# Stores behind later loads, and side work re-spread, in a decoder layer on one core

## Chip, cores and metric

One core of a Trainium2 chip runs the whole layer in one launch. The time is device microseconds from start to end of that launch; lower is better. Three runs of the kernel before took 2120.0, 2126.58 and 2126.95 us.

## What is computed

One decoder layer over 2048 tokens of width 1024 in fp32, shortened from the reference:

```python
mod = silu(c) @ w_ada + b_ada                       # 6 x 1024
h = rms_norm(x, g_mix) * (1 + scale1) + shift1
z, q, k, v = split(h @ w_in)                        # 1024 | 512 | 128 | 128
u, v_a = split(gelu(z)); out_a = u * (tril(w_s) applied per 128-token chunk to v_a, + b_s)
out_b = attention(rope(q), rope(k), v)              # window 128, 8 heads, 2 kv heads, sinks
x = x + gate1 * (concat(out_a, out_b) @ w_out)
h2 = rms_norm(x, g_ffn) * (1 + scale2) + shift2
x = x + gate2 * (relu(h2 @ w_ff1) ** 2 @ w_ff2)     # 1024 -> 4096 -> 1024
y = rms_norm(x, g_final)
```

## The kernel before

**Tiles.** The tokens go in four slabs of 512, features on the partitions. Every fp32 operand of a large product is split into a rounded part and a remainder (hi, lo), and each product of 128 x 128 by 128 x 512 is three matmuls (mm3, L298 to L300): hi hi, hi lo, lo hi. Splitting is one ACT pass (hi) and one DVE pass (lo): halve (L69, L70) and w_split (L265, L266).

**Order of the program.** The slabs pass through the input projection (in_qkv for q, k, v; in_vu for the gated unit), attention, mix_build (reading both mixers' outputs back and splitting them), out_proj, and the MLP. The MLP takes slabs in pairs (0, 1) and (2, 3) and uses a seven-product scheme in place of eight blocks: h2_build makes seven forms of the normalised activations, ffn_c the first product (16 feature blocks j of 7 products), ffn_d the second (products 1, 6, 5, 3, 7, 4, 2, each over 8 contraction steps c, so 56 steps of 24 matmuls). w2_early and w2_late form sums of blocks of the second weight and keep them in DRAM (w2d). ada_rest computes a later part of the modulation vector in halves of 512 outputs: eight loaded slices, each scaled by ACT (L168) and added by POOL (L170), then four matmuls of one column.

**Weaving.** Each stage is a generator. weave(main, side, per) runs `per` steps of the side after each step of the main; ratio, chain, zipped and part combine side generators. What is written in this order, each engine's instructions then stand in an order that a scheduler sets; issue_after makes one instruction stand behind another. Before, the first pair's ffn_d runs three side steps per c step: slab 2's attention, all of slab 3 up to its out_proj, then h2_build of the second pair; w2_late takes one step per c step from the fifth on.

**Queue and buffers.** All large transfers are issued by SP, in program order; an issue waits for its data (a store) or for a free buffer (a load), and what stands behind it waits too. Stores are issued where the data is made: split weights (w_keep, L278), mixer outputs (L538, L654), residuals (L690), q, k, v of slabs 2 and 3 (L414), the weight sums (L770 to L786). Tiles come from rings: t2 (9 of 512 columns), xl (4), wk (12 of 1024), m2 (60). Statistics of a slab are a column sum by matmul (L201), a power on POOL (L206), and a broadcast by matmul (L221).

Of the kernel before, what the change touches and what calls it, by code (L numbers as in the profile page):

```python
# [49 lines left out]
def hybrid_block(ctx, tc, x_l, c_l, pos, wada0, wada, vec, win, wsT, bs, sinks, wout, w1, w2, rope_c, y_l):  # L50
# [54 lines left out]
    def x_tile(s, k, tag_x=False):  # L105
        t = m2("xr", F32) if tag_x else sb.tile([P, T], F32, name="xt", tag="xl", bufs=NXL)
        nc.sync.dma_start(out=t, in_=x_l[s, k])
        return t
# [51 lines left out]
    def ada_rest(ci):  # L160
        for half in range(2):
            acc = t2("acc")
            for k in range(KT):
                if k % 2 == 0:
                    two = wk("adar", F32, [P, 2, T])
                    nc.sync.dma_start(out=two, in_=wada[ci - 2, half, k:k + 2].rearrange("k p t -> p k t"))
                raw = two[:, k % 2]
# [87 lines left out]
    def w_split(key, big=False, eng=dve):  # L255
        raw = wk("raw", F32)
        nc.sync.dma_start(out=raw, in_=(win if key[0] == "i" else wout)[key[1]])
# [15 lines left out]
    def w_keep(key, w):  # L273
        n = D // len(w.hi)
        kept[key] = [dram.tile([P, D], F32, name=f"k{key[0]}{key[1]}{q}", tag=f"k{key[0]}{key[1]}{q}") for q in "hl"]
        for d, ts in zip(kept[key], (w.hi, w.lo)):
            for i, t in enumerate(ts):
                nc.sync.dma_start(out=d[:, i * n:(i + 1) * n], in_=t.bitcast(F32))  # L278

    def w_load(key):  # L280
# [3 lines left out]
        for t, d in zip((hi, lo), kept[key]):  # L284
            nc.sync.dma_start(out=t.bitcast(F32), in_=d)
# [40 lines left out]
    def setup_mixers():  # L326
        for i in range(2):
# [8 lines left out]
            for t in (wh, wl):  # L336
                wspd.append(dram.tile([P, T], F32, name=f"wsp{len(wspd)}", tag=f"wsp{len(wspd)}"))
                nc.sync.dma_start(out=wspd[-1], in_=t.bitcast(F32).rearrange("p g c -> p (g c)"))
# [73 lines left out]
    def away(s, name, t):  # L412
        d = dram.tile([P, T], F32, name=f"{name}d{s}", tag=f"{name}d{s}")
        nc.sync.dma_start(out=d, in_=t)  # L414
        qkvd[s, name] = d

    def back(s, name, t):
        nc.sync.dma_start(out=t, in_=qkvd[s, name])
# [67 lines left out]
    def in_vu(s, h, st, u0=None):  # L486
        vts, us = {}, {}
        sgu = list(wsp)
        if s > 0:
            ts = [m2("wsp", F32R, [P, 4, P]) for _ in range(4)]  # L490
            for t, d in zip(ts, wspd):
                nc.sync.dma_start(out=t.bitcast(F32).rearrange("p g c -> p (g c)"), in_=d)
# [27 lines left out]
        def gate(p):  # L520
# [17 lines left out]
            nc.sync.dma_start(out=mixd[s][p], in_=sv)  # L538
# [19 lines left out]
    def attention(s, st):  # L558
# [82 lines left out]
        def stage_o(n):  # L641
# [4 lines left out]
            for i, (kb, pt) in enumerate(pts):  # L646
                for hl in range(2):
# [6 lines left out]
            nc.sync.dma_start(out=mixbd[s][:, a:a + HD, b * P:(b + 1) * P].rearrange("j p c -> p j c"),  # L654
                              in_=os_[a:a + HD])
# [14 lines left out]
    def mix_build(s, mix):  # L670
        for k in range(KT):
            t = sb.tile([P, T], F32, name="xt", tag="xl", bufs=NXL)
            nc.sync.dma_start(out=t, in_=mixd[s][k] if k < 4 else mixbd[s][k - 4])
# [7 lines left out]
    def out_proj(s, mix):  # L681
        stat = Stat()
        for d in range(KT):
# [6 lines left out]
            nc.sync.dma_start(out=x2d[s][d], in_=x2)  # L690
# [21 lines left out]

    def h2_build(p, forms):
        for s in (2 * p, 2 * p + 1):
            rb2[s].diag()
        yield
        for s in (2 * p, 2 * p + 1):
            rb2[s] = rb2[s].cast()
        yield
        def leaf(kk, t):  # L720
            xt = sb.tile([P, T], F32, name="xt", tag="xl", bufs=NXL)
            nc.sync.dma_start(out=xt, in_=x2d[2 * p + t][kk])
# [3 lines left out]
            act.activation(out=b, in_=b, func=AF.Identity, bias=mod[:, 3 * KT + kk:3 * KT + kk + 1])  # L726
            return b
# [6 lines left out]

        for k in range(4):
            b11, b21 = leaf(k, 0), leaf(k + 4, 0)
            keep_form(1, b11)
            keep_form(2, b21)
            yield
            b12, b22 = leaf(k, 1), leaf(k + 4, 1)  # L740
# [14 lines left out]
    def w2_quarter(o, c, dp, f0):  # L755
        nc.sync.dma_start(out=o.rearrange("p (a m) -> p a m", a=2),
                          in_=w2[4 * c + dp].rearrange("p (a m) -> p a m", a=2)[:, :, f0 * P:(f0 + 2) * P])
# [5 lines left out]

    def w2_early():
        for n in range(16):
            c, dp = divmod(n, 2)
            cs = slice(dp * T, (dp + 1) * T)
            a21, a22, a11 = w2_half("a21", c, dp + 2, 0), w2_half("a22", c, dp + 2, 2), w2_half("a11", c, dp, 0)
            dve.tensor_tensor(out=a22, in0=a21, in1=a22, op=ALU.add)
            nc.sync.dma_start(out=w2d[5, c][:, cs], in_=a22)  # L770
            dve.tensor_tensor(out=a11, in0=a22, in1=a11, op=ALU.subtract)
            nc.sync.dma_start(out=w2d[6, c][:, cs], in_=a11)
            yield

    def w2_late():
        for n in range(16):
            c, dp = divmod(n, 2)
            cs = slice(dp * T, (dp + 1) * T)
            a12 = w2_half("a12", c, dp, 2)
            s2 = sb.tile([P, T], F32, name="s2", tag="xl", bufs=NXL)  # L780
            nc.sync.dma_start(out=s2, in_=w2d[6, c][:, cs])
            dve.tensor_tensor(out=a12, in0=a12, in1=s2, op=ALU.subtract)
            nc.sync.dma_start(out=w2d[3, c][:, cs], in_=a12)
            a11, a21 = w2_half("a11", c, dp, 0), w2_half("a21", c, dp + 2, 0)
            dve.tensor_tensor(out=a21, in0=a11, in1=a21, op=ALU.subtract)
            nc.sync.dma_start(out=w2d[7, c][:, cs], in_=a21)  # L786
# [11 lines left out]
    def ffn_c(p, forms):  # L798
# [42 lines left out]
        for j in range(16):  # L841
# [5 lines left out]
            if j == 0:  # L847
                product(j, 2, x, False)
                b11 = relu2(t2("b11"), x)
# [39 lines left out]
    def ffn_d(p, last):  # L889
# [4 lines left out]
        def fetch(src, r, t):  # L894
            for b in range(4):
                if src is x2d:
                    xs[r, t, b] = m2("x3", F32)
                else:
                    two = wk("x3w", F32, [P, 2, T]) if b % 2 == 0 else two
                    xs[r, t, b] = two[:, b % 2]  # L900
                nc.sync.dma_start(out=xs[r, t, b],
                                  in_=x2d[2 * p + t][4 * r + b] if src is x2d else src[r, t, b])
# [18 lines left out]
        for i in (1, 6, 5, 3, 7, 4, 2):  # L921
# [5 lines left out]
            for c in range(8):  # L927
# [5 lines left out]
                else:  # L933
                    nc.sync.dma_start(out=wraw, in_=w2d[i, c])
                nc.sync.dma_start(out=araw, in_=ad[p, i, c])
# [43 lines left out]
    def final_norm(s, xs, t, stat):  # L979
# [6 lines left out]
        for d in range(KT):  # L986
            x = xs[d // 4, t, d % 4]
            if x is None:
                x = sb.tile([P, T], F32, name="xt", tag="xl", bufs=NXL)
                nc.sync.dma_start(out=x, in_=x3d[d // 4, t, d % 4])  # L990
# [12 lines left out]
    def weave(main, side, every=1, per=1):  # L1003
        n = 0
        for _ in main:
            n += 1
            if n % every == 0:
                for _ in range(per):
                    step(side)
# [66 lines left out]

    ada = [ada_first_load(0)]
# [34 lines left out]
    feed(range(NPRE))  # L1112
    sts = [{} for _ in range(NSLAB)]
# [138 lines left out]
```

## Time and profile before

| | |
|---|---|
| runs | 2120.0, 2126.58, 2126.95 us |
| profiled execution | 2121.88 us, of which the span of the trace is 2120.2 us |
| busy: PE, DVE, ACT, POOL | 1930, 1424, 949, 243 us |
| mean granted TensorE clock | 0.959 |
| DMA | 478 MB, 226 GB/s over the span |

A busy time says how long an engine had an instruction in it. PE is the engine that has most, so the profile is read by asking in which stretches PE is idle or runs at the lower granted clock, and what it waited for there. A granted clock of 1.00 is 2.4 GHz; the lower level is 1.2 GHz, and a window's figure is a mean of the two.

### The profile page before, as it was taken

To read this page: it belongs to the slowest core of one execution; us is meant where nothing else is said; L and a number is where in the kernel's file an instruction comes from. 1 tells how busy PE (TensorE), PEld (TensorE's weight loads), DVE (VectorE), ACT (ScalarE), POOL (GpSimd) and SP (SyncE) were. 2 spreads that over 40 slices of the span, in tenths; PEclk is the share of its full clock that TensorE was granted. 3 is DMA by queue.
4 is the path that set the end of the run, shared out by engine and by line. 5 is a ranking of instruction groups with operands and counts; after the bars stand their busy time and mean duration, and the time that the engine had idled before them with its cause. 6 is when DMAs were issued, how large, how long until landed. Compare 5 with 4: busy or idle time off the path is not lost. (4 is left out here: it accounts for less than half of the span.)

```text
span 2120.2 us, 25995 instructions
## 1 busy us (share of the span) xinstructions
PE 1930.0 (91%) x8852; PEld 1586.7 (75%) x8852; DVE 1423.8 (67%) x2342; ACT 949.4 (45%) x1621; POOL 242.5 (11%) x290
## 2 busy tenths in 40 slices
PE   4798879899699999989998997988999999999997
PEld 3687757678577888767886886866888888888875
DVE  5579858846887766687556584677866665554675
ACT  3354645514554544543344353345444444443442
POOL 2416301230220000011010122000000000000000
PEclk9899989999799999999998998999999999999998
DMA  8887577594797444889976767576444436556663
GB/s 309 276 305 254 172 238 260 168 369 176 235 321 283 164 150 164 277 291 307 350 253 210 246 206 248 194 251 203 143 160 150 164 137 213 199 187 217 232 213 131
DMA packets 231605, 478.38 MB, mean 226 GB/s; under 512 B 23296, under 2 KB 80768, under 8 KB 231472
## 3 DMA queue, kind: packets, MB, share of 16 engines
q1 hardware_dynamic: 230352, 475.99, 65.6%
q8 instruction: 70, 1.15, 0.2%
q0 software_dynamic: 1120, 0.72, 0.1%
q14 instruction: 63, 0.52, 0.1%
HBM read 345.35 MB, written 131.27 MB: 225 GB/s over the span
## 5 line engine op out<-in xcount | busy, mean ns | idle before, releaser
L299 PE MATMUL mm<-al,w2h 128*128 128x512 f32 x896 | 358.4, 400 | 13.9 <-DVE al L70 13.8
L300 PE MATMUL mm<-ah,w2l 128*128 128x512 f32 x896 | 354.9, 396 | 0.0
L298 PE MATMUL mm<-ah,w2h 128*128 128x512 f32 x896 | 316.9, 400 | 19.4 <-ACT ah L69 17.4
L69 ACT ACTIVATE w2h<-w2w 128x1024 fp32r<-128x1024 f32 x112 | 118.7, 1060 | 313.0 <-DMA w2w<-w2d 133.6
L70 DVE TENSOR_TENSOR w2l<-w2w,w2h 128x1024 fp32r<-128x1024 f32 x112 | 139.0, 1241 | 167.8 <-ACT w2h L69 160.2
L299 PEld LDWEIGHTS mm<-al,w2h 128*128 128x128 f32 x896 | 172.3, 192 | 57.6 <-DVE al L70 22.6
L298 PEld LDWEIGHTS mm<-ah,w2h 128*128 128x128 f32 x896 | 170.2, 191 | 58.6 <-ACT ah L69 21.4
L300 PEld LDWEIGHTS mm<-ah,w2l 128*128 128x128 f32 x896 | 172.2, 192 | 35.3
L70 DVE TENSOR_TENSOR al<-aw,ah 128x1024 fp32r<-128x1024 f32 x112 | 137.8, 1230 | 33.4 <-ACT ah L69 23.2
L206 POOL TENSOR_TENSOR rs<-ms,mhalf 128x4 f32<-128x4 f32 x12 | 13.5, 1123 | 1200.3 <-DVE ms L204 908.8
L298 PE MATMUL mm<-h,whi 128*128 128x512 f32 x320 | 128.2, 416 | 20.6 <-ACT h L236 7.8
L69 ACT ACTIVATE ah<-aw 128x1024 fp32r<-128x1024 f32 x112 | 118.5, 1058 | 58.5 <-DMA aw<-ad 22.5
L299 PE MATMUL mm<-h,whi 128*128 128x512 f32 x320 | 130.4, 409 | 7.4 <-DVE h L237 7.4
L300 PE MATMUL mm<-h,wlo 128*128 128x512 f32 x320 | 129.0, 405 | 1.2 <-POOL wlo L266 1.2
L298 PE MATMUL mm<-hw,wah 128*128 128x512 f32 x256 | 102.8, 403 | 19.0 <-ACT hw L731 10.3
L298 PE MATMUL mm<-mix,whi 128*128 128x512 f32 x256 | 104.9, 412 | 16.0 <-ACT mix L675 12.9
L299 PE MATMUL mm<-mix,whi 128*128 128x512 f32 x256 | 104.0, 407 | 3.5 <-DVE mix L676 3.5
L299 PE MATMUL mm<-hw,wah 128*128 128x512 f32 x256 | 102.5, 400 | 2.6 <-DVE hw L732 2.6
L300 PE MATMUL mm<-hw,wal 128*128 128x512 f32 x256 | 101.9, 399 | 0.8 <-DVE wal L70 0.8
L300 PE MATMUL mm<-mix,wlo 128*128 128x512 f32 x256 | 102.6, 401 | 0.0
L298 PE MATMUL mm<-hw,wbh 128*128 128x512 f32 x256 | 99.8, 390 | 0.9 <-DVE w L857 0.9
L299 PE MATMUL mm<-hw,wbh 128*128 128x512 f32 x256 | 99.8, 390 | 0.0
(258 smaller groups left out, 4403.0 us busy)
## 6 DMA issues: line engine op xcount, KB each, us to landing
aw<-ad SPq DMA_DIRECT2D x112, 512.0 KB, 5.1
r<-in_w_dram SPq DMA_DIRECT2D x64, 512.0 KB, 4.8
w2w<-w2d SPq DMA_DIRECT2D x64, 512.0 KB, 3.9
a<-in_w_dram SPq DMA_DIRECT2D x96, 256.0 KB, 4.9
ad<-wt SPq DMA_DIRECT2D x96, 256.0 KB, 2.1
w2w<-in_w_dram SPq DMA_DIRECT2D x96, 256.0 KB, 3.8
xt<-in_x_dram SPq DMA_DIRECT2D x80, 256.0 KB, 5.2
adar<-in_wada_dram SPq DMA_DIRECT2D x32, 512.0 KB, 6.9
```

The source lines that it names most:

```text
L69: act.activation(out=hi, in_=t, func=AF.Copy)
L70: dve.tensor_tensor(out=lo, in0=t, in1=hi, op=ALU.subtract)
L206: self.pow = pool.tensor_tensor(out=rs[:, :nb], in0=ms[:, :nb], in1=mhalf[:, :nb], op=ALU.pow)
L298: pe.matmul(out=out, lhsT=wh, rhs=h[0], start=first, stop=False, **kw)
L299: pe.matmul(out=out, lhsT=wh, rhs=h[1], start=False, stop=False, **kw)
L300: last_mm[0] = pe.matmul(out=out, lhsT=wl, rhs=h[0], start=False, stop=last, **kw)
```

## The change

A store is no longer issued where its data is made. put() lists it, and get(), through which nearly all loads now go, issues listed stores behind the second load after them; a load of something still listed issues it first. Before the first weights are all in (hold), none is issued. ada_rest's products are multiply-adds on DVE, with ACT only for the first of eight. w2_late is cut in two, one sum per step, and the sums begin at the third c step; w2_early and ada_rest(5) start after 14 steps of ffn_c. h2_build first makes all eight leaves of the pair's even slab (forms 1 and 2), keeps them in DRAM (h2d), and reads them back for the mixed forms; for the first pair that early part runs beside out_proj(1), for the second between mix_build(3) and out_proj(3). Side steps per main step change, and slab 2's statistics move beside attention. In ffn_c the first feature block has an own bank for product 2.

```diff
+    def put(dst, out, in_):
+        pend.append([0, dst, out, in_])
+    def emit(n, ins=None):
+        for _ in range(n):
+            _, _, out, in_ = pend.pop(0)
...
+                with tc.issue_after(ins.ins):
+                    nc.sync.dma_start(out=out, in_=in_)
+    def get(out, in_, src=None):
+        known = [i for i, p in enumerate(pend) if p[1] is src]
+        if src is not None and known:
+            emit(known[-1] + 1)
+        ins = nc.sync.dma_start(out=out, in_=in_)
+        if not hold[0]:
+            for p in pend:
+                p[0] += 1
+            emit(sum(p[0] > 1 for p in pend), ins)
+        return ins
...
-                act.activation(out=raw if k else acc, in_=raw, func=AF.Copy, scale=cact[:, k:k + 1])
+                raw, sc = two[:, k % 2], cact[:, k:k + 1]
                 if k:
-                    pool.tensor_tensor(out=acc, in0=acc, in1=raw, op=ALU.add)
+                    dve.scalar_tensor_tensor(out=acc, in0=raw, scalar=sc, in1=acc, op0=ALU.mult, op1=ALU.add)
+                else:
+                    act.activation(out=acc, in_=raw, func=AF.Copy, scale=sc)
...
-                nc.sync.dma_start(out=d[:, i * n:(i + 1) * n], in_=t.bitcast(F32))
+                put(d, d[:, i * n:(i + 1) * n], t.bitcast(F32))
...
+        rb2[2 * p].diag()
+        yield
+        rb2[2 * p] = rb2[2 * p].cast()
+        yield
+        for kk in range(KT):
+            b = leaf(kk, 0)
+            keep_form(1 if kk < 4 else 2, b)
+            put(h2d[p, kk], h2d[p, kk], b)
+            yield
+        yield "even"
...
         for k in range(4):
-            b11, b21 = leaf(k, 0), leaf(k + 4, 0)
-            keep_form(1, b11)
-            keep_form(2, b21)
-            yield
-            b12, b22 = leaf(k, 1), leaf(k + 4, 1)
+            b11, b12 = again(k), leaf(k, 1)
+            b21, b22 = again(k + 4), leaf(k + 4, 1)
...
             if j == 0:
-                product(j, 2, x, False)
-                b11 = relu2(t2("b11"), x)
+                q2, b11 = bank("mm"), t2("b11")
+                product(j, 2, q2, True)
+                dve.tensor_tensor(out=b11, in0=q2, in1=p1, op=ALU.add)
+                relu2(b11)
...
-          ratio(chain(then_halo(0, attention(0, st)), mix_build(0, mix), x_stats(2, rn), spread(rn)), 5,
-                part(ada, 6), 1), per=3)
+          ratio(chain(then_halo(0, attention(0, st)), mix_build(0, mix)), 3,
+                chain(part(ada, 6), x_stats(2, rn), spread(rn)), 1), per=3.5)
...
-run(out_proj(1, mix1))
+weave(out_proj(1, mix1), until(h2, "even"), per=1.3)
...
-    weave(in_vu(2, hx, sts[2]), h2)
+    weave(in_vu(2, hx, sts[2]), h2, per=1.5)
...
-    weave(ffn_c(0, forms), chain(ada_rest(5), w2_early()), every=3)
+    for n, _ in enumerate(ffn_c(0, forms)):
+        if n > 13 and n % 5 == 0:
+            step(w2f)
+        if n > 13 and n % 9 == 1:
+            step(ada)
...
-        yield from chain(mix_build(3, m3_), out_proj(3, m3_))
+        yield from mix_build(3, m3_)
+        yield from until(h2, "even")
+        yield from out_proj(3, m3_)
...
-        if 4 <= n:
-            step(w2l)
-        for _ in range(3):
+        if 2 <= n < 22:
+            step(s4 if n < 18 else s3)
+        elif n < 30:
+            step(s3)
+            step(s3)
+        for _ in range(4):
             more = step(side)
```

**Where instructions now stand.** SP, from about the tenth microsecond of the program. `raw` is a weight as loaded, `ki8h` and `ki8l` are its kept parts; lines differ because the changed file is longer. Before:

```order
L354 DMA ropec<-in_ropec_dram 128x1
L278 DMA ki8h<-whi 128x1024
L257 DMA raw<-in_win_dram 128x1024
L278 DMA ki8l<-wlo 128x1024
L278 DMA ki9h<-whi 128x1024
L257 DMA raw<-in_win_dram 128x1024
L278 DMA ki9l<-wlo 128x1024
L278 DMA ki10h<-whi 128x1024
L257 DMA raw<-in_win_dram 128x1024
L278 DMA ki10l<-wlo 128x1024
L278 DMA ki11h<-whi 128x1024
L257 DMA raw<-in_win_dram 128x1024 x3
```

After, the six loads stand together, and the stores come in a row further down:

```order
L382 DMA ropec<-in_ropec_dram 128x1
L93 DMA raw<-in_win_dram 128x1024 x6
L159 DMA ada_566<-in_wada_dram 128x512
L159 DMA ada_568<-in_wada_dram 128x512
...
L86 DMA ki0h<-whi 128x1024
L93 DMA raw<-in_win_dram 128x1024
L86 DMA ki8h<-whi 128x1024
L86 DMA ki8l<-wlo 128x1024
L86 DMA ki9h<-whi 128x1024
L86 DMA ki9l<-wlo 128x1024
```

Between the two pieces after stand sixteen modulation loads and the first loads of the next stage; before, those modulation loads stood behind the stores of six and of seven weights.

DVE in out_proj(1), some of its eight groups: `x` is the new residual, `ssum` its sum of squares, `hb` a normalised leaf, `hw` the low part of a form. Before:

```order
L687 SCALAR_TENSOR_TENSOR x_4487<-mm,mod,xt 128x512
L195 TENSOR_TENSOR ssum<-ssum,sq 128x512
L177 TENSOR_TENSOR mod<-modp,vecs 128x4
L181 SCALAR_TENSOR_TENSOR gs<-mod,vecs 128x8
L687 SCALAR_TENSOR_TENSOR x_4524<-mm,mod,xt 128x512
L195 TENSOR_TENSOR ssum<-ssum,sq 128x512
L687 SCALAR_TENSOR_TENSOR x_4561<-mm,mod,xt 128x512
L195 TENSOR_TENSOR ssum<-ssum,sq 128x512
```

After:

```order
L715 SCALAR_TENSOR_TENSOR x_4448<-mm,mod,xt 128x512
L223 TENSOR_TENSOR ssum<-ssum,sq 128x512
L762 TENSOR_TENSOR hw<-hb,hw 128x512
L749 SCALAR_TENSOR_TENSOR hb<-xt,gs,rbc 128x512
L762 TENSOR_TENSOR hw<-hb,hw 128x512
L749 SCALAR_TENSOR_TENSOR hb<-xt,gs,rbc 128x512
L762 TENSOR_TENSOR hw<-hb,hw 128x512
L715 SCALAR_TENSOR_TENSOR x_4505<-mm,mod,xt 128x512
L223 TENSOR_TENSOR ssum<-ssum,sq 128x512
L749 SCALAR_TENSOR_TENSOR hb<-xt,gs,rbc 128x512
L715 SCALAR_TENSOR_TENSOR x_4552<-mm,mod,xt 128x512
L223 TENSOR_TENSOR ssum<-ssum,sq 128x512
```

The leaves and forms of slab 0 now stand between the residuals of slab 1; before, they stood behind all of them.

PE in in_vu(2), where slab 1's statistics end (`msp` is the column sum, `bcp` the broadcast). Before, slab 0's broadcast stands behind 21 matmuls of 256 columns, and slab 1's behind 26 more:

```order
L509 MATMUL mm<-whi,h 128x256
L201 MATMUL msp<-ones,ssum 128x1 x4
L510 MATMUL mm<-whi,h 128x256
...
L509 MATMUL mm<-whi,h 128x256
L221 MATMUL bcp<-dg,ones_r 128x512 x2
L510 MATMUL mm<-whi,h 128x256
...
L511 MATMUL mm<-wlo,h 128x256
L221 MATMUL bcp<-dg,ones_r 128x512 x2
L509 MATMUL mm<-whi,h 128x256
```

After, the first broadcast stands directly behind the sums:

```order
L327 MATMUL mm<-h,whi 128x512
L328 MATMUL mm<-h,wlo 128x512
L229 MATMUL msp<-ones,ssum 128x1 x4
L249 MATMUL bcp<-dg,ones_r 128x512
L326 MATMUL mm<-h,whi 128x512
L327 MATMUL mm<-h,whi 128x512
```

Slab 0's broadcast now stands in out_proj(1).

## Rows read from the trace of the kernel before

**Rows 1.** The page, part 1: busy us, share of the span, instructions

```profile
PE 1930.0 (91%) x8852; PEld 1586.7 (75%) x8852; DVE 1423.8 (67%) x2342; ACT 949.4 (45%) x1621; POOL 242.5 (11%) x290
```

**Rows 2.** Windows by stage; columns as in their heading line

```profile
core 0: us, PE busy (x) PEld busy (x) DVE busy (x) ACT busy (x) POOL busy (x), PEclk, DMA share, GB/s
0.00:94.00 94.00, 58.99 (x210) 44.60 (x210) 52.87 (x84) 25.12 (x38) 41.70 (x71) 0.89 0.86 297
94.00:158.00 64.00, 56.72 (x353) 51.72 (x352) 48.44 (x83) 40.18 (x68) 8.09 (x12) 0.95 0.85 296
158.00:281.00 123.00, 104.08 (x598) 90.17 (x598) 100.24 (x229) 72.50 (x175) 59.21 (x62) 0.94 0.64 219
281.00:326.00 45.00, 30.69 (x116) 24.09 (x117) 26.56 (x48) 18.07 (x34) 1.04 (x1) 0.81 0.78 243
326.00:523.00 197.00, 183.79 (x945) 152.78 (x944) 134.82 (x303) 86.79 (x210) 47.65 (x58) 0.97 0.69 246
523.00:626.00 103.00, 80.35 (x332) 62.54 (x332) 89.55 (x121) 52.83 (x82) 21.78 (x14) 0.88 0.77 259
863.00:1364.00 501.00, 459.18 (x2145) 376.76 (x2144) 327.75 (x647) 206.80 (x429) 57.52 (x67) 0.96 0.76 260
1364.00:1500.00 136.00, 118.53 (x475) 93.33 (x474) 105.15 (x147) 67.47 (x93) 3.52 (x4) 0.91 0.58 198
1500.00:1790.00 290.00, 290.00 (x1281) 240.13 (x1280) 192.89 (x266) 138.89 (x200) 0.00 (x0) 1.00 0.48 164
```

**Rows 3.** SP's queue in order of time: start us, length us, operation

```profile
19.62 0.33 SPq L257 DMA_DIRECT2D raw<-in_win_dram  x1
...
27.20 0.42 SPq L257 DMA_DIRECT2D raw<-in_win_dram  x1
...
32.84 0.42 SPq L257 DMA_DIRECT2D raw<-in_win_dram  x1
...
39.09 1.78 SPq L257 DMA_DIRECT2D raw<-in_win_dram  x3
...
59.86 4.77 SPq L132 DMA_DIRECT2D ada<-in_wada_dram  x8
```

**Rows 4.** What SP's queue waited for: total us, times, longest us

```profile
SPq L278 <- ACT whi L265: 58.0, 19, 6.4
...
SPq L654 <- DVE os L653: 59.1, 21, 10.1
```

**Rows 5.** Groups by line (POOL, ACT, DVE), and POOL's and DVE's timeline about 160

```profile
L170 POOL TENSOR_TENSOR acc<-acc,adar 128x512 f32<-128x512 f32 x56 | 81.6, 1471 | 153.4 <-ACT acc L168 123.1 <-ACT adar L168 28.5 <-POOL acc L170 0.3
...
L168 ACT ACTIVATE adar<-adar,cact 128x512 f32<-128x512 f32 x56 | 37.5, 714 | 21.1 <-DMA adar<-in_wada_dram 18.9 <-DMA q0d<-qr 2.0
...
157.86 12.67 POOL L170 TENSOR_TENSOR acc<-acc,adar 128x512 f32<-128x512 f32 x8
...
163.44 3.44 DVE L237 SCALAR_TENSOR_TENSOR h<-ht,mod,h 128x512 fp32r<-128x512 f32 x2
...
L687 DVE SCALAR_TENSOR_TENSOR x<-mm,mod,xt 128x512 f32<-128x512 f32 x32 | 23.9, 748 | 46.5 <-PE mm L300 45.7 <-DMA xt<-in_x_dram 0.7
...
L732 DVE TENSOR_TENSOR hw<-hb,hw 128x512 fp32r<-128x512 f32 x32 | 21.1, 687 | 0.4 <-ACT hw L731 0.2
...
L70 DVE TENSOR_TENSOR w2l<-w2w,w2h 128x1024 fp32r<-128x1024 f32 x112 | 139.0, 1241 | 167.8 <-ACT w2h L69 160.2 <-PE mm L299 5.9 <-PE mm L300 1.2
...
L70 DVE TENSOR_TENSOR al<-aw,ah 128x1024 fp32r<-128x1024 f32 x112 | 137.8, 1230 | 33.4 <-ACT ah L69 23.2 <-issue 7.8 <-DMA mixb<-os 1.1
```

**Rows 6.** PE's timeline at four gaps; in brackets the idle time before it

```profile
311.97 1.84 PE L201 MATMUL msp<-ones,ssum 128*128 128x1 f32 x8 [5.16 <-DVE ssum L195]
...
318.58 1.30 PE L221 MATMUL bcp<-dg,ones_r 128*128 128x512 f32 x2 [4.77 <-DVE dg L215]
...
539.50 0.80 PE L298 MATMUL mm<-hw,wah 128*128 128x512 f32 x1 [7.27 <-ACT hw L731]
...
1485.65 0.80 PE L298 MATMUL mm<-hw,wah 128*128 128x512 f32 x1 [3.92 <-ACT p L846]
```

More of the change, by code (lines that the diff above doesn't have):

```diff
@@ L256, in w_split @@
         raw = wk("raw", F32)
-        nc.sync.dma_start(out=raw, in_=(win if key[0] == "i" else wout)[key[1]])
+        get(raw, (win if key[0] == "i" else wout)[key[1]])
         if big:
@@ L1005, in weave @@
         for _ in main:
[L1006 to L1009, printed above, removed]
+            n += per / every
+            while n >= 1:
+                n -= 1
+                step(side)
         for _ in side:
@@ L1126, in hybrid_block, with until @@
         ada = chain(ada_rest(2), ada_rest(3), ada_rest(4))
-        weave(in_vu(0, h, st, u0), chain(x_stats(1, rb), spread(rb), h_build(1, rb, hn), part(ada, 6)), per=2)
+        weave(in_vu(0, h, st, u0), chain(x_stats(1, rb), spread(rb), h_build(1, rb, hn)), per=2)
+    def until(g, mark):
+        for v in g:
+            if v == mark:
+                return
+            yield
     def ratio(a, na, b, nb):
@@ L1148, in hybrid_block @@
     weave(chain(in_qkv(1, hn, st1), in_vu(1, hn, st1)),
[L1149 to L1150 removed]
+          ratio(chain(then_halo(0, attention(0, st)), mix_build(0, mix)), 3,
+                chain(part(ada, 6), x_stats(2, rn), spread(rn)), 1), per=3.5)
     att = then_halo(1, attention(1, st1))
[L1152 removed]
+    weave(out_proj(0, mix), part(ratio(ratio(att, 3, h_build(2, rn, hx), 1), 7, ada, 1), 40), per=4.5)
     rope_load(2)
[L1154 to L1155 removed]
+    weave(in_qkv(2, hx, sts[2]), ratio(chain(att, mix_build(1, mix1)), 2, ada, 1), per=3.5)
     ada_gs()
@@ L1168, in beside @@
         rope_load(3)
-        yield from zipped(chain(qkv_back(2, st2), late(attention, 2, st2)),
+        yield from zipped(chain(qkv_back(2, st2), then_halo(2, late(attention, 2, st2)), late(qkv_back, 3, st3)),
                           chain(x_stats(3, rb3), h_build(3, rb3, h3), in_qkv(3, h3, st3), in_vu(3, h3, st3)))
-        keep_halo(2)
-        yield from qkv_back(3, st3)
         yield from zipped(attention(3, st3), chain(mix_build(2, m2_), out_proj(2, m2_)))
-        yield from chain(mix_build(3, m3_), out_proj(3, m3_))
+        yield from mix_build(3, m3_)
+        yield from until(h2, "even")
+        yield from out_proj(3, m3_)
     def late(f, *a):
         yield from f(*a)
-    side, w2l, h2 = beside(), w2_late(), h2_build(1, forms1)
+    side, h2, s4, s3 = beside(), h2_build(1, forms1), w2_late(3), w2_late(7)
     last = []
     for n, _ in enumerate(ffn_d(0, last)):
-        if 4 <= n:
-            step(w2l)
-        for _ in range(3):
+        if 2 <= n < 22:
[4 more added lines that the diff above has]
+        for _ in range(4):
             more = step(side)
@@ L1187, in hybrid_block @@
             step(h2)
-    run(side, w2l, h2)
+    run(side, h2)
     weave(ffn_c(1, forms1), last[0])
@@ L1191, in hybrid_block @@
     run(last[1])
+    emit(len(pend))
 def _layout(inputs):
```

98 lines of the change are left out of this document (54 added, 44 removed).

## The prediction

> **What bounds the kernel now.** Three views, in this order. The page's engine list first: PE is busy 1930 us of 2120, DVE 1424 [rows 1], so the matmuls set the time wherever they are fed. Then a table of windows cut by stage [rows 2], to see where they are not. In 1500 to 1790 PE runs 1281 matmuls in 290 us at full clock, 0.2264 us each; that is the price of a fed matmul, and 24 of them (one contraction step of the second MLP product, a "c step") cost 5.43 us. For any other window I call lost what PE idled plus the window times (1 - granted clock), since a matmul at the lower clock takes twice as long. Lost: 35.0 + 10.3 = 45 us in 0 to 94, 10 in 94 to 158, 26 in 158 to 281, 23 in 281 to 326, 19 in 326 to 523, 35 in 523 to 626, 62 in 863 to 1364, 30 in 1364 to 1500. The change can win only there; all of it is some 250 us. Third, what PE waited for at the largest gaps, and what SP's queue waited for, below.
>
> **Start, 0 to 158: stores leave the queue.** SP issues in order. Before, the store of a split weight stands ahead of the next weight's load and waits for ACT's split: the second and third weight's loads go out at 19.6 and 27.2 us and the last three from 39.1, the last eight modulation loads only from 59.9 to 64.6, to land 5.6 later [rows 3]; over the run SP waits 58 us at that store (L278) and 59 at L654 [rows 4]. After, six weight loads and sixteen modulation loads follow one another, and the stores come behind, 27 of them in a row (first order fences). Loads needed up to the last modulation product are 14.2 MB (8 and 32 tiles of 256 KB, 7 of 512 KB); at 297 GB/s [rows 2] that is 48 us, against 64.6 + 5.6 = 70 now: about 20 us sooner at best. But in the new order PE has all of its last 84 matmuls (19 us) behind the last modulation product where it had 48 (11 us), so 8 of the 20 go back: **-12**. Ends: -20; and +5, if the 10 MB of postponed stores (29 us at 345 GB/s, which is 297 over the share of 0.86), now ahead of three weight loads, make the 94 to 158 stretch wait.
>
> **Modulation product on DVE, 158 to 281.** It removes 56 POOL adds (1.47 us each) and 56 ACT scalings (0.71), and adds 56 DVE multiply-adds, 0.75 us each by the nearest row, 42 us [rows 5]. What did a POOL add cost DVE? From 157.9 POOL runs eight in 12.7 us, and the DVE passes beside them take 1.72 us where such a pass takes 0.75 [rows 5]: about 1 us of DVE per add. So the swap is no load for DVE; in a busy place it gives 0.25 us back per product, and all of ACT's. Two of the four half-products that lay from 150 to 281 move on to later stages: of 28 adds (up to 28 us of DVE's 100 busy in 123) 14 multiply-adds remain (10.5 us). PE waited there on h, the very passes that were stretched. I take a third of the 26 lost: **-8**; ends -14 and +3.
> The Trainium skill, "SBUF — State Buffer", section "SBUF: two separate sides", says that DVE with two SBUF inputs and GpSimd take one port pair as an exclusive lock, the loser blocked for the whole instruction. By that 28 adds would cost DVE 28 x 1.47 = 41 us and the term would be nearer -14; the rows agree in kind and show about 1 us.
>
> **Statistics of slab 2, 281 to 326.** Two waits, 5.2 us at the column sums (L201) and 4.8 at the broadcast (L221) that stands directly behind [rows 6]; the chain ends behind mix_build. Now the statistics run beside the attention, and the order has 36 matmuls between sum and broadcast, 8 us. Both waits go, with part of the low clock (0.81): **-12** of 23; ends -16 and -3.
>
> **Stage 326 to 523.** It gets the even slab's 8 normalisations and 8 splits, 8 x (0.75 + 0.69) = 11.5 us of DVE [rows 5], and the rest of the moved products; DVE was busy 135 of 197 [rows 2], so that is covered; were DVE full, it would cost all 11.5. What is late next: the last order fence has slab 1's first broadcast right behind its column sums, where 47 short matmuls and slab 0's broadcast stood between. That is the shape that cost 4.8 us [rows 6]: **+5**; ends 0 and +12.
>
> **Entry of the MLP, 523 to 626.** Before, h2_build has 18 steps, in_vu(2) offers 9, two go ahead, and seven run alone: 7.3 us at the worst gap [rows 6], with DVE 87% busy [rows 2]. After, 14 steps are left for 9 x 1.5, so no more than one runs alone, and the modulation and weight sums start only at the 14th step of the product. **-22** of 35; ends -30 and -8.
>
> **Second MLP product of the first pair, 863 to 1500.** The side work goes from 3 to 4 steps per c step: about 122 steps over 41 c steps become about 132 over 33. Matmul work of the side part: 501 - 62 = 439, less 8 c steps of 5.43, 395 us. DVE there: 328 busy, less 8 x 2.47 (L70's two passes [rows 5]), less one product's folds (about 11), plus 11.5: 308, or 78% of 395, where it was 65% of 501. The one weight sum per step instead of two, and no store ahead of a load, speak for fewer waits, the density for more. It lost 13% before, and 158 to 281 lost 21% at 81% DVE; I take 14.5%: 395 / 0.855 = 462, plus 43.5 for the 8 c steps that now come later, less 501: **+4**. Ends: 8% lost, -28; 21%, +42. Behind it, h2_build of the second pair ran over the last 15 c steps with DVE busy 105 of 136 and lost 30; now 14 lighter steps spread over 23: **-15**, ends -25 and -3.
>
> **First feature block's own bank.** The second product no longer waits for ACT's copy of the first; that wait was 3.9 us [rows 6], once per pair: **-3** together with the two extra DVE adds (0.69 each); ends -5 and 0. The final stores and the tail stay.
>
> **Sum.** -12 - 8 - 12 + 5 - 22 + 4 - 15 - 3 = -63. The profiled execution took 2121.9 us: 2059. The median of the three runs shown, 2126.6, is 4.7 above it; with the same offset I predict **2064**.
>
> **Rivals.**
> *The good ends.* Start -20, products -12, statistics -15, stage +2, entry -28, side part -28, tail of the product -22, bank -4: -127, giving 2000. For it: low clock goes with idling in every lossy window [rows 2], so a gap closed pays twice. Against: DVE stays above 75% in three of them.
> *Given back to DMA.* Between the first and the last x2d1 store the order now has 51 DMAs, 18.4 MB by their shapes, before 34 and 14.2. At 345 GB/s that is 53 us beside seven groups' 38: +12 over before; and the side part at 18% lost instead of 14.5 adds 20. -31: 2096. Against it: the mean of 326 to 523 is 246 GB/s.
> *DVE pays in full.* Had the POOL adds cost DVE nothing, 42 multiply-adds up to 523 add 31 us where DVE is busy 235 of 320 us, and the -8 goes: -24, 2103. Rows 5 speak against it.
> The Trainium skill, "Perfetto Trace Analysis", section "Optimizing Scalar/DVE Operations", says that with DVE saturated some work may be better moved to Scalar or even GpSimd, and adds that GpSimd shares DVE's read port; its first half is this rival's rule and speaks against the change.
> *Slower: the side part becomes DVE's.* At 4 steps per c step DVE is the bound and PE falls to the lower clock, as in 523 to 626, which lost 34% at 87% DVE [rows 2]. 395 / 0.66 = 598, +141 in place of +4: 2201. It turns the whole into a loss from 25% lost on. Against it: 78% is what I count, not 87.
> *Not what it says.* The scheduler could have left the order alone; the fences show that it did not.
>
> **Chances.** Forecast 0.55 (its own range 2035 to 2090), good ends 0.15, DMA 0.14, DVE in full 0.07, slower side part 0.09. A measurement here tells about 0.5% from no change, 10.6 us. Within that fall 0.01 of the forecast, 0.01 of the DMA case, 0.02 of the DVE case and 0.02 of the last: 0.06. Slower: 0.07 of the last case. Faster: 0.87. The range 2005 to 2105 leaves out half of the good ends and the slower case.
>
> **What would show it.** Right: the four weight loads issued within some 10 us, modulation done by 50 to 60; DVE passes of 0.75 around 160; no idle above 5 us at L201 and L221 except the one behind slab 1's sums; PE over 90% busy where the MLP begins; the second product's side part at about 460 us. Wrong: DVE above 85% with PE under 80% there, or PE waiting on weight loads in out_proj(1) and in_vu(0).

## The result, and the profile after

The changed kernel takes 2096.41 us (median of four runs, 2087.11 to 2100.68), the kernel before 2125.89 on the same chip (2120.0 to 2126.95): ratio 0.9861, 95% interval 0.9822 to 0.9900. It is faster, as forecast, but by 29.5 us where 62 were forecast. The profiled execution is the fastest of the four, 2087.1 us, 34.8 below the one before; the steps of the forecast are held against it.

The page, part 1, of the changed kernel (as [rows 1]):

```profile
PE 1917.2 (92%) x8852; PEld 1581.0 (76%) x8852; DVE 1419.1 (68%) x2400; ACT 914.2 (44%) x1565; POOL 170.9 (8%) x234
```

Windows of the changed kernel (columns as in [rows 2]). They are cut near the points of [rows 2], not all at the same ones: 263 to 306, for one, lies later in out_proj(0) than 281 to 326 did. 483 to 822 is all of the first MLP product, cut into two. Of the kernel before, [rows 2] leaves out the stretch that 586 to 822 is held against, which stands last here:

```profile
0.00:76.00 76.00, 52.21 (x214) 41.25 (x214) 55.41 (x84) 26.23 (x39) 45.34 (x71) 1.00 0.95 333
143.00:263.00 120.00, 108.45 (x619) 94.25 (x618) 97.19 (x260) 71.42 (x178) 28.02 (x37) 0.94 0.59 203
263.00:306.00 43.00, 40.54 (x200) 33.00 (x198) 35.11 (x87) 19.74 (x55) 4.36 (x6) 1.00 1.00 362
306.00:483.00 177.00, 155.67 (x793) 130.58 (x792) 132.69 (x285) 72.42 (x167) 26.86 (x39) 0.95 0.81 292
483.00:586.00 103.00, 97.07 (x428) 80.04 (x427) 77.93 (x115) 48.34 (x72) 0.00 (x0) 0.97 0.50 170
586.00:822.00 236.00, 223.51 (x970) 182.47 (x970) 161.29 (x231) 101.06 (x148) 0.00 (x0) 0.98 0.71 241
822.00:1308.00 486.00, 434.63 (x2010) 354.88 (x2009) 313.10 (x636) 204.29 (x433) 52.53 (x67) 0.94 0.76 259
1308.00:1451.00 143.00, 128.16 (x544) 101.93 (x543) 103.02 (x134) 65.79 (x81) 4.32 (x3) 0.96 0.71 237
```

```profile
626.00:863.00 237.00, 235.19 (x1036) 194.08 (x1036) 159.01 (x222) 111.13 (x161) 0.00 (x0) 1.00 0.59 202
```

By the forecast's measure (idle time of PE plus the time lost to the lower clock) 103 us from 483 lose 9 us where 103 us from 523 lost 35, and hold 428 matmuls for 332. From 586 on that is given back: 17 lost for 2 up to ffn_d, and 81 for 62 in the next row. Before 483 one stretch is worse as well; it is shown further down. Between marks that both traces have (first transposed weight on PE, last residual of out_proj(0) and of out_proj(1), first matmul of ffn_d, first matmul of the second pair's MLP, end), the lengths are:

| from, to | before | after | forecast | measured |
|---|---|---|---|---|
| 0, first transpose | 94.3 | 75.5 | -12 | -19 |
| to the end of out_proj(0) | 278 | 255 | -8 -12 | -23 |
| to the end of out_proj(1) | 100 | 102 | 0 | +2 |
| to ffn_d, first pair | 390 | 389 | +5 -22 | -1 |
| to the second pair's MLP | 616 | 629 | +4 -15 | +13 |
| to its ffn_d | 310 | 304 | -3 | -6 |
| to the end | 331 | 331 | 0 | 0 |

The +5 stands in the fourth row because the wait that it forecast comes 15 us after the end of out_proj(1). Two rows fall short, by 16 and by 24 us, one by 2; three others are better than forecast by 13 together. That is, but for rounding, the 28 us by which the profiled execution (2087) lies above the sum (2059). The median lies 9 above the profiled execution.

SP's queue at the start, in order of time (as [rows 3]): the six loads and the sixteen modulation loads go out by 41.2, the stores from 52.65.

```profile
18.93 11.53 SPq L93 DMA_DIRECT2D raw<-in_win_dram  x6
30.51 10.72 SPq L159 DMA_DIRECT2D ada<-in_wada_dram  x16
...
52.65 0.33 SPq L86 DMA_DIRECT2D ki0h<-whi  x1
```

DVE's timeline, and a DVE group by line, where [rows 5] had POOL's adds and passes of 1.72 us: a multiply-add takes 0.75 and the pass behind it 0.69.

```profile
156.38 0.75 DVE L196 SCALAR_TENSOR_TENSOR acc<-adar,cact,acc 128x512 f32<-128x512 f32 x1
157.05 0.69 DVE L433 TENSOR_TENSOR qs<-qs,S_t 128x512 f32<-128x512 f32 x1
```

```profile
L196 DVE SCALAR_TENSOR_TENSOR acc<-adar,cact,acc 128x512 f32<-128x512 f32 x56 | 41.7, 745 | 6.8 <-DMA adar<-in_wada_dram 4.6 <-ACT acc L198 1.8
```

PE at the statistics of slab 2 and behind slab 1's sums (as [rows 6]; idle time before an instruction in brackets, where there was any). The 5.16 and 4.77 are gone, and the predicted new wait is there with 3.10, in in_vu(2):

```profile
260.86 0.95 PE L229 MATMUL msp<-ones,ssum 128*128 128x1 f32 x8
270.42 0.39 PE L249 MATMUL bcp<-dg,ones_r 128*128 128x512 f32 x1
...
448.74 0.47 PE L249 MATMUL bcp<-dg,ones_r 128*128 128x512 f32 x1 [3.10 <-DVE dg L243]
```

That wait is part of a larger loss, and the rest of it stood in no term of the forecast. The 50 us from the end of out_proj(1), which are in_vu(2), were full before; now, with h2_build woven in at 1.5 steps instead of one and the broadcast among them, they lose 11 us, and the MLP's first matmul comes 55.6 us after the end of out_proj(1) where it came after 50.0. Before, then after:

```profile
473.00:523.00 50.00, 50.00 (x330) 46.06 (x330) 31.52 (x55) 24.05 (x39) 1.22 (x2) 1.00 0.56 195
```

```profile
433.00:483.00 50.00, 43.69 (x258) 39.39 (x257) 29.74 (x52) 19.80 (x33) 1.60 (x2) 0.90 0.68 239
```

**What the two short rows show.** The weight sums (w2_early) were to begin at the 14th step of ffn_c. In the order that the scheduler made, the first four loads-and-sums stand much earlier and their stores don't. DVE's timeline, the first four sums, L812 and L814:

```profile
482.31 0.68 DVE L812 TENSOR_TENSOR a<-a,a 128x512 f32<-128x512 f32 x1
486.14 0.69 DVE L814 TENSOR_TENSOR a<-a,a 128x512 f32<-128x512 f32 x1
491.39 0.69 DVE L812 TENSOR_TENSOR a<-a,a 128x512 f32<-128x512 f32 x1 [0.28 <-DMA a<-in_w_dram]
497.51 0.68 DVE L814 TENSOR_TENSOR a<-a,a 128x512 f32<-128x512 f32 x1
```

SP's timeline, all of its transfers of `a` from 476 to 562, and the two modulation loads among them:

```profile
476.59 2.86 SPq L93 DMA_DIRECT2D a<-in_w_dram  x2
...
483.02 0.54 SPq L93 DMA_DIRECT2D a<-in_w_dram  x1
...
484.88 7.76 SPq L93 DMA_DIRECT2D a<-in_w_dram  x3
...
551.13 1.49 SPq L93 DMA_DIRECT2D adar<-in_wada_dram  x2
552.67 0.94 SPq L86 DMA_DIRECT2D w2d<-a  x2
...
558.61 0.55 SPq L93 DMA_DIRECT2D a<-in_w_dram  x1
...
559.89 0.55 SPq L93 DMA_DIRECT2D a<-in_w_dram  x1
...
561.13 0.90 SPq L86 DMA_DIRECT2D w2d<-a  x2
```

Each sum stays in one of the four xl tiles until it is stored, so from 498 to 552 all four tiles hold finished sums, and no load of `a` goes out from 493 to 558. A store comes behind two later loads, and these two were modulation loads at 551. Windows of 20 to 40 us: the DMA queues stand at a quarter where PE enters the MLP, and at 0.80 to 0.87 later, where the other 28 sums crowd into ffn_c and PE pays.

```profile
500.00:520.00 20.00, 17.36 (x65) 13.72 (x66) 15.68 (x22) 8.75 (x11) 0.00 (x0) 0.83 0.22 71
520.00:540.00 20.00, 20.00 (x90) 16.58 (x89) 12.97 (x18) 9.65 (x14) 0.00 (x0) 1.00 0.42 133
...
640.00:680.00 40.00, 34.89 (x145) 28.32 (x144) 29.65 (x43) 14.52 (x21) 0.00 (x0) 0.91 0.80 272
680.00:720.00 40.00, 36.17 (x160) 28.73 (x158) 26.95 (x41) 16.28 (x24) 0.00 (x0) 1.00 0.87 292
```

PE's largest gap there, and ACT behind it: ACT waited 5.79 us for a weight block `r`. SP issued that load at 643.77, behind two loads of `a` at 641.00.

```profile
653.47 0.79 PE L326 MATMUL mm<-hw,wah 128*128 128x512 f32 x1 [5.11 <-ACT p L889]
```

```profile
650.70 1.06 ACT L69 ACTIVATE wah<-r 128x1024 fp32r<-128x1024 f32 x1 [5.79 <-DMA r<-in_w_dram]
```

SP's waits over the whole run, in the form of [rows 4], four of the rows: the wait of a load for a tile whose sum's store has still to land (72.8 us; before, the rows of this kind are 36.4, 5.5, 4.3 and 3.3), and one that is new, of a load for a tile of the ring into which an early sum is still being read back for w2_late. Of the 72.8 us, 28.7 lie between out_proj(1) and ffn_d and 44.1 in ffn_d, as do the 20.4; in run 11 below it is 18.0 and 26.7, and there is no row for the read-back. The waits at the mixer outputs and split weights fell, from 59.1 to 39.0 and from 58.0 to 8.9.

```profile
SPq L93 <- DMA w2d<-a: 72.8, 38, 5.2
SPq L86 <- DVE os L681: 39.0, 15, 11.8
SPq L93 <- DMA s<-w2d: 20.4, 6, 5.3
SPq L86 <- ACT whi L293: 8.9, 3, 4.8
```

### The profile page after: what moved, and what is told of

Its sections match the earlier page's. It is cut to its first block, busy times and chain, and to the rows that moved or that the text cites. A ratio compares the mean times of both kernels' runs of the same rounds, so it can differ in the third digit from the quotient of the medians.

```text
span 2085.4 us, 25949 instructions
## 1 busy us (share of the span) xinstructions
PE 1917.2 (92%) x8852; PEld 1581.0 (76%) x8852; DVE 1419.1 (68%) x2400; ACT 914.2 (44%) x1565; POOL 170.9 (8%) x234
## 4 chain that ended last, share of the span: by engine, by line
PE 47%; DMA 9%; DVE 6%; ACT 2%; issue 1%; SPq 1%; POOL 0%; POOLq 0%; DVEq 0%; ACTq 0%
PE mm L327 15%; PE mm L328 15%; PE mm L326 15%; DMA aw<-ad 3%; DMA xt<-in_x_dram 1%; DVE al L70 1%; DMA w2w<-in_w_dram 1%; DMA xt<-x2d 1%; ACT ah L69 1%; DVE w2l L70 1%; DMA w2w<-w2d 1%; DMA xt<-mixb 1%; SPq L93 1%; DVE x L950 1%; DMA w2d<-a 1%
## 5 line engine op out<-in xcount | busy, mean ns | idle before, releaser
L326 PE MATMUL mm<-h,whi 128*128 128x512 f32 x320 | 126.1, 406 | 9.7 <-ACT h L264 6.1
L327 PE MATMUL mm<-h,whi 128*128 128x512 f32 x320 | 128.3, 402 | 1.6 <-DVE h L265 1.6
L234 POOL TENSOR_TENSOR rs<-ms,mhalf 128x4 f32<-128x4 f32 x12 | 17.7, 1473 | 1355.1 <-DVE ms L232 1342.3
L326 PE MATMUL mm<-hw,wdh 128*128 128x512 f32 x256 | 99.8, 390 | 2.2 <-DVE w L912 2.2
L326 PE MATMUL mm<-hw,wbh 128*128 128x512 f32 x256 | 99.7, 389 | 0.0
```

Of the source, the lines that this page charges most:

```text
L234: self.pow = pool.tensor_tensor(out=rs[:, :nb], in0=ms[:, :nb], in1=mhalf[:, :nb], op=ALU.pow)
L326: pe.matmul(out=out, lhsT=wh, rhs=h[0], start=first, stop=False, **kw)
L327: pe.matmul(out=out, lhsT=wh, rhs=h[1], start=False, stop=False, **kw)
```

## The experiments

The theories. **A, the ring**: the postponed stores of the weight sums hold the four xl tiles and, by SP's order, the loads behind them. **B, density**: four side steps per c step crowd DVE. **C, the spread**: one late sum per c step over 28 steps disturbs more of them than two over fewer. **D, the read-back**: slab 3's q, k and v come back in the side part beside slab 2's. **E**: late stores and denser sums together starve the ring. Ratios are to the kernel before, run on the same chip (medians 2119.6 for the first four, 2123.3 for the next four, 2120.35 for the last four). The changed kernel has its own measurement of the kernel before (2125.89), so runs are held against it by their ratios (its own: 0.9861, 0.9822 to 0.9900). Lengths of a stage are from the profiled execution of each kernel, one for each, and so only as good as that.

**1. The modulation product alone**, put into the kernel before.

```diff
-                raw = two[:, k % 2]
-                act.activation(out=raw if k else acc, in_=raw, func=AF.Copy, scale=cact[:, k:k + 1])
+                raw, sc = two[:, k % 2], cact[:, k:k + 1]
...
-                    pool.tensor_tensor(out=acc, in0=acc, in1=raw, op=ALU.add)
+                    dve.scalar_tensor_tensor(out=acc, in0=raw, scalar=sc, in1=acc, op0=ALU.mult, op1=ALU.add)
```

> The kernel before, with nothing but the modulation product moved to DVE. If a POOL add really takes about 1 us of DVE, the swap is free for DVE and frees ACT: 5 to 12 us faster than before (2114 to 2121). If POOL's adds cost DVE nothing, 42 us of DVE come on top: up to 31 us slower, 2126 to 2157. The DVE passes on h after in_vu(0) fall from 1.75 us to 0.75 under the first, and stay under the second.

2102.61 us, 0.9926 (0.9901 to 0.9951): 17 us by the medians, more than the 5 to 12 expected; the interval reaches down to 10. From the first transpose to the end of out_proj(0) it takes 259 us, 19 fewer than before. In this window DVE is as busy as in 158 to 281 of [rows 2], and PE gets 629 matmuls into 119 us where it had 598 in 123:

```profile
163.00:282.00 119.00, 109.35 (x629) 94.63 (x629) 97.65 (x261) 66.36 (x167) 24.61 (x36) 0.96 0.70 243
```

The passes on h take 0.75 us, as expected, where they took 1.72 [rows 5]:

```profile
155.48 0.75 DVE L238 SCALAR_TENSOR_TENSOR h<-ht,mod,h 128x512 fp32r<-128x512 f32 x1
```

From 94 to 282 PE's waits for DVE's pr and h fall from 8.6 and 5.2 us to 0.3 and 0.9. That speaks for DVE as the place of the gain; the freed ACT has no run of its own, and DVE's wait for ACT's es fell too, from 10.5 to 2.6. Why the gain is twice the forecast is open.

Of the two prices weighed for this term, -8 from the rows and -14 by the rule of the Trainium skill ("SBUF — State Buffer", section "SBUF: two separate sides") that the loser of the port is blocked for the whole instruction, the second came nearer.

**2. The sums stored at once**, all else as changed.

```diff
-        put(w2d[i, c], w2d[i, c][:, dp * T:(dp + 1) * T], t)
+        nc.sync.dma_start(out=w2d[i, c][:, dp * T:(dp + 1) * T], in_=t)
```

> The changed kernel, but the stores of the second weight's sums (w2d) are issued where the sum is made, as before. Theory A, the ring: the postponed stores keep the four xl tiles, SP's queue waits for them and holds up everything behind it, in ffn_c of the first pair above all. Then ffn_c there, 333 us from 489 to 822, gets 10 to 15 us shorter and the whole comes to 2081 to 2087 where the changed kernel has 2096. Rival, DVE's extra work or the spacing of the sums does it: no change, 2092 to 2100, and the waits for ACT's copy p stay.

2080.17 us, 0.9808 (0.9777 to 0.9838): by the ratios some 11 us faster than the changed kernel, but the intervals overlap. From out_proj(1) to ffn_d 385 us (389), ffn_d 624 (629). This speaks for A, and for less of it than expected: ffn_c, which was to get 10 to 15 us shorter, takes 328 for 333. The wait of loads for sums falls from 72.8 to 56.0 us, and the read-back's is gone.

```profile
SPq L93 <- DMA w2d<-a: 56.0, 44, 3.9
```

**3. Three side steps per c step again.**

```diff
-        for _ in range(4):
+        for _ in range(3):
```

> The changed kernel with three side steps per contraction step in the second product of the first pair, as before, in place of four. Theory B, density: the stage, 629 us in the changed kernel and 616 before, comes back to 610 to 616, the whole to 2077 to 2086. Rival: the stage is set by what the stores and the DMA order do and not by the density: 625 to 635, no change; or the tail of the product with h2_build grows again by more than the side part gains: 2100 or more.

2099.76 us, 0.9908 (0.9878 to 0.9938): no faster than with four, and ffn_d takes 630 us for 629; the stretch behind it, into which h2_build now reaches, takes 312 for 304. The side part runs over 46 c steps in place of 34 and loses 16% of its time, as with four. B falls: the density costs nothing that fewer steps give back.

**4. All stores at once**, with everything else of the change.

```diff
-        pend.append([0, dst, out, in_])
+        nc.sync.dma_start(out=out, in_=in_)
```

> The changed kernel with every store issued where its data is made, all else as changed. By theory A ffn_c of the first pair gets its 10 to 15 us back, and the start loses the 18 us that it gained: 2095 to 2105 in all. If the postponed stores help the second product too, more than that: 2110 or above. If they only harm outside the start: 2085 to 2095.

2089.95 us, 0.9855 (0.9824 to 0.9887), the same as the changed kernel, and in the range of the third case, that late stores only harm outside the start. The first transpose is at 93 us again (75.5 with late stores), but out_proj(1) to ffn_d takes 383 and ffn_d 625. So postponing gains some 18 us at the start and, by the medians, nothing as a whole; in the two profiled executions these two stages pay back 10 of the 18.

**5. A fifth xl tile**, stores late as changed.

```diff
-NT, NM, NWK, NXL = 9, 60, 12, 4
+NT, NM, NWK, NXL = 9, 59, 12, 5
```

> The changed kernel with five tiles in the xl ring in place of four, and 59 instead of 60 in the m2 ring to make room. If the ring is what the postponed stores starve, ffn_c of the first pair falls from 310 us (first to last stage mark) towards the 298 of the kernel with its sums stored at once, and the second product of the first pair, 629 us, falls by 5 to 15: 2070 to 2085 in all on a chip where the changed kernel takes some 2090. Rival: the waits came from the order of the queue alone, then a fifth tile moves less than 5 us.

2087.5 us, 0.983 (0.9806 to 0.9855). The interval overlaps that of the changed kernel, and ffn_d is no shorter (632). A fifth tile alone gives nothing that can be seen: again four finished sums stand from 495 to 553, the fifth tile holds one more loaded block beside them, and SP waits for sums 84.3 us instead of 72.8.

**6. The late sums left out.**

```diff
-                    get(wraw, w2d[i, c], w2d[i, c])
+                    w_s = w2d[{3: 6, 7: 5}.get(i, i), c]
+                    get(wraw, w_s, w_s)
...
-    side, h2, s4, s3 = beside(), h2_build(1, forms1), w2_late(3), w2_late(7)
+    side, h2, s4, s3 = beside(), h2_build(1, forms1), iter(()), iter(())
```

> The changed kernel without w2_late: products 3 and 7 of the second pair of feature halves read the sums 6 and 5 instead, so 32 sums (64 loads, 32 stores, 32 DVE passes, some 24 us of DVE and 25 MB) leave the second product of the first pair, and the output is not the reference's. If loads through the queue and the ring bound that stage, it falls from 629 by 20 to 40 us. If DVE does, by its 24 us times the share in which it is the last to come, 5 to 15. If the latencies of attention and mix_build do, by less than 5.

2056.06 us, 0.9688 (0.9672 to 0.9704); ffn_d takes 600 us, 29 fewer. That is the whole price of the late sums there, for 32 sums of 0.69 us of DVE with their 64 loads and 32 stores, and it lies in the range that was written for loads through the queue and the ring. What remains in ffn_d without them is 600 against the 605 that the forecast had with them.

**7. Without the early forms of the second pair.**

```diff
-        yield from until(h2, "even")
```

> The changed kernel without the even slab's forms between mix_build(3) and out_proj(3); they come after out_proj(3), ahead of the mixed forms, at one step per contraction step. By my prediction the early forms take 15 us out of the tail of the second product, so this is 10 to 15 us slower than the changed kernel, 2100 to 2105. Rival: the stage loses in its side part what it wins in its tail, then 0 to 5 either way, and the time from the last residual of slab 2 to the first of slab 3, 100 us, shrinks to about 85 while the tail grows by as much.

2103.95 us, 0.9916 (0.9889 to 0.9942). ffn_d takes 647 us, 18 more, so in the changed kernel the early forms are worth their place. That is not yet the -15 of the forecast, which was against the kernel before. There the tail, from the last residual of slab 3 to the second pair's MLP, lost 22 us:

```profile
1364.00:1479.00 115.00, 101.45 (x410) 79.58 (x409) 84.93 (x115) 56.40 (x76) 2.20 (x3) 0.93 0.67 227
```

It loses 21 in the changed kernel (1308 to 1451) and 31 in this run. Most of the 15 did not come.

**8. Stored at once, and five tiles**: the edits of 2 and 5.

> The candidate for best: the sums stored at once and a fifth xl tile. If both act on the same wait, no more than 3 us below the kernel with the sums stored at once (2080); if the ring also holds up attention's and mix_build's loads in the second product, 5 to 12 below, 2068 to 2075.

2069.43 us, 0.9755 (0.9721 to 0.9789). Out_proj(1) to ffn_d takes 381 us, ffn_d 616. Against run 5, on the same chip and with the same five tiles, nothing differs but the stores of the sums: 18 us, with intervals far apart. This is the clearest proof of what the late stores cost. Against run 2 a tile more seems worth its place with the stores at once, but those intervals overlap a little.

**9. Both late sums in each c step**, from the fifth on, as before the change; stores late.

```diff
-        if 2 <= n < 22:
-            step(s4 if n < 18 else s3)
-        elif n < 30:
-            step(s3)
+        if 4 <= n:
+            step(s4)
```

> The changed kernel with both late sums in each of sixteen contraction steps from the fifth on, as before, stores still behind later loads. The second product and the first product after it take 933 us together in the changed kernel, 926 before, and I had forecast 912. Theory C, the spread of the sums over 28 steps, up to two per step where attention and out_proj run, costs what went missing: 915 to 925 and 2075 to 2085 in all. Rival D, the mixers of slab 3 begun early: no change, 930 to 938. Rival E, the ring: denser sums with late stores starve it more, 940 or above.

2095.49 us, 0.9873 (0.9852 to 0.9895); ffn_d 638, and 942 for the two products, as E said. C falls: bringing the sums together doesn't help while their stores are late.

**10. Slab 3's read-back after slab 2's attention**, stores late.

```diff
-        yield from zipped(chain(qkv_back(2, st2), then_halo(2, late(attention, 2, st2)), late(qkv_back, 3, st3)),
+        yield from zipped(chain(qkv_back(2, st2), late(attention, 2, st2)),
...
+        keep_halo(2)
+        yield from qkv_back(3, st3)
```

> The changed kernel with keep_halo(2) and qkv_back(3) after the zipped stretch, as before. Theory D, q, k and v of slab 3 read back and split in the middle of attention 2's end and in_vu(3) cost the side part: 915 to 925 for the two products and 2075 to 2085 in all. Rival C or E: no gain, and the gap where attention 3 begins, which the early read-back was to fill, grows by some 5 us: 935 to 940.

2088.71 us, 0.9846 (0.9829 to 0.9863); ffn_d 630 for 629, the two products 934. No gain: D falls.

**11. The edits of 8 and 9 together.**

> The kernel with sums stored at once and five xl tiles (2069), with both late sums per step as before. By theory C 5 to 15 us faster than it, 2055 to 2064. By E no loss here either, since its stores are not late: 2065 to 2073, and the difference to the same edit with late stores is then the cost of the late stores alone.

2065.89 us, **0.9738 (0.971 to 0.9766)**: the best version found, faster than both kernels. Out_proj(1) to ffn_d takes 380 us, ffn_d 612. The same edit as in 9 lengthened ffn_d by 9 us with late stores and doesn't here, as E says; between 8 and 11 the intervals overlap. SP's and DVE's timelines show the ring at work; each store follows its sum within a microsecond:

```profile
483.30 0.68 DVE L812 TENSOR_TENSOR a<-a,a 128x512 f32<-128x512 f32 x1
485.11 0.68 DVE L814 TENSOR_TENSOR a<-a,a 128x512 f32<-128x512 f32 x1
```

```profile
484.01 0.33 SPq L806 DMA_DIRECT2D w2d<-a  x1
484.39 0.55 SPq L93 DMA_DIRECT2D a<-in_w_dram  x1
485.82 0.32 SPq L806 DMA_DIRECT2D w2d<-a  x1
```

Its windows: the sums now load the DMA queues from 480 to 600, beside the entry, where PE loses 19 us for the 9 of the changed kernel (the largest gap is 7.08 us at 507.56), and PE is full from 586 to ffn_d, where the changed kernel loses 17. The last two rows are its side part of ffn_d, which loses 61 us for 81, and the tail behind it.

```profile
485.00:586.00 101.00, 88.97 (x382) 71.89 (x382) 84.89 (x130) 42.95 (x66) 0.00 (x0) 0.93 0.89 300
586.00:814.00 228.00, 228.00 (x1015) 188.98 (x1015) 155.78 (x216) 109.77 (x158) 0.00 (x0) 1.00 0.55 189
814.00:1279.00 465.00, 431.43 (x2011) 354.74 (x2010) 314.24 (x636) 201.89 (x432) 53.84 (x67) 0.94 0.78 273
1279.00:1427.00 148.00, 130.02 (x549) 102.38 (x548) 104.06 (x135) 65.92 (x81) 4.32 (x3) 0.97 0.68 228
```

**12. The edits of 8 and 10 together.**

> The kernel with sums stored at once and five xl tiles (2069), with slab 3's read-back as before. By theory D 5 to 15 us faster, 2055 to 2064; by the rivals 2069 to 2076.

2076.98 us, 0.9791 (0.977 to 0.9812): no faster than 8. D falls here as well.

## Why the prediction was half right

**The start** (-12): -19. The stores left the queue as forecast, and the last modulation product came 28 us sooner (52.7 for 81.3), not 20. The matmuls that wait behind it, 84 for 48, took back 10, as charged with 8. Run 4 ties the gain to the late stores: without them the first transpose is at 93.

**Modulation product** (-8) **and statistics** (-12): -23 together, and run 1 gives 19 of it to the product alone. The direction holds, and so, by PE's waits in run 1, does the reason (POOL's adds hold DVE); the product was worth more than twice its 8, and the statistics about a third of their 12: in run 1, where they have not moved, their two waits still stand with 5.8 and 2.5 us, and the stretch is only 4 us longer than in the changed kernel. That the two terms come near their sum is luck. The rival that DVE pays in full is out.

**Stage with the new broadcast** (+5): the wait came with 3.10 where 4.8 was the row, and in_vu(2), where it stands, took 5.6 us longer. The forecast had it in 326 to 523, which held the same part of in_vu(2). Out_proj(1) itself took 2 more.

**Entry of the MLP** (-22): this is the first failed step. As the prediction put it, the sums "start only at the 14th step of the product", and what 626 to 863 would lose by them was put at nothing. The entry itself gained: from the first matmul of the MLP, 103 us lose 9 for 35. But in the scheduler's order four sums stood at its very start, held the ring for 54 us, and the other 28 came all together behind them, so 586 to 822 lost 17 for 2. From the MLP's first matmul to ffn_d that leaves 6 us of the 22. With the stores at once the sums run beside the entry, and from the end of out_proj(1) the stretch takes 385 (run 2), 381 (run 8) and 380 (run 11) for 389: the ring explains up to 9 of the 16 that are missing in that row. The sums beside the entry then cost PE there.

**Side part of ffn_d** (+4): the second failed step, "no store ahead of a load" as a point for fewer waits. The rows of before showed that a store in the queue makes later loads wait; that a store behind loads keeps its tile, and so makes the same loads wait on a ring of four, was costed at nothing. The side part lost 81 us (51.4 idle and 29 by the clock) where it had lost 62 and the forecast's 14.5% are 67. It also ended after 34 c steps, from 40 before, where the forecast had 33 and 41; and what it lost before is 12%, not 13. Storing the sums at once, with a fifth tile, brings ffn_d from 629 to 616, with both sums per step to 612, and there the side part loses 61, no more than before the change.

**The tail behind it** (-15): the third. "Lost 30" was read over 1364 to 1500, of which the last 21 us are already the next stage; the tail itself had lost 22. It lost 21 after the change, and 22 in run 11. Run 7 shows that without the early forms it would be worse, not that they beat the kernel before; what else holds the tail is open.

**Own bank** (-3): -6, of which the wait of 3.92 [rows 6] is gone.

**The rivals.** The DMA case gave 2096, which is the result, but not its cause. Its 38 to 53 us of transfers around slab 1's residuals cost +2, not +12. The side part did lose 16.6% (18% in that rival), yet run 11 moves 273 GB/s there against 259 and takes 465 us for 486: the queues had room, and with the tiles freed sooner that room was used. The side part did not become DVE's either: DVE is busy 313 of 486 us, and fewer steps give nothing back (run 3).

**What stays open.** Run 11's profiled execution (2063) is 4 above the sum of 2059, but not by its terms: the start and the bank gave 9 more, the stretch to ffn_d and ffn_d itself 7 less each. Why the changed kernel's own runs spread over 13 us, and what else the entry lost of its 22 (the gap of 7.08 at a weight split is one piece), was not settled. No kernel held the sums back until the 14th step in the scheduler's order too.

## What to carry over

Before you postpone a store, ask which buffer it keeps and how many such there are: here, a store on a ring of four or five tiles was best issued at once, even though it makes the queue wait, while a store from tiles that nobody soon needs can go behind the loads. Count what is held, not only what is passed in the queue, and read from the instruction order, not from the source, when the held work begins. A gain in a stage is only there once the work that it pushed out has been paid for.

## What the runs showed of the hardware

An add with two inputs on POOL takes DVE about 1 us, an estimate from these rows, and more than the same work done on DVE: DVE passes of 0.75 us took 1.72 beside it [rows 5], and taking 56 adds of 1.47 us from POOL, and their scalings from ACT, onto DVE (41 us of it) made the kernel 17 us faster, with no other edit. Both wait: an add with no DVE pass beside it took 1.28 us, those beside the passes of 1.72 took 1.7. It was not every DVE pass that suffered. While POOL added without a pause from 433 to 445 in the kernel before, a pass with one of its inputs in PSUM (`mm`) took its usual 0.75, and a pass with two in SBUF took 3.34 where its mean is 0.73:

```profile
438.13 0.75 DVE L687 SCALAR_TENSOR_TENSOR x<-mm,mod,xt 128x512 f32<-128x512 f32 x1 [4.77 <-PE mm L300]
439.58 3.34 DVE L195 TENSOR_TENSOR ssum<-ssum,sq 128x512 f32<-128x512 f32 x1 [0.70 <-ACT sq L191]
```

Full DMA queues alone did not slow the matmuls here: in run 11, 540 to 600, they were busy 1.00 at 352 GB/s while PE ran 59.2 of 60 us at full clock.

```profile
540.00:600.00 60.00, 59.21 (x261) 48.68 (x261) 50.34 (x75) 28.61 (x43) 0.00 (x0) 1.00 1.00 352
```
